# Queueing the last products behind the last transposes, and splitting the last row tile in three pieces, in a trace-of-product kernel

## The chip, the cores and the metric

One core of a Trainium2 chip runs the kernel. The metric is the device time of the whole program in microseconds (us); medians of repeated runs are quoted with their range. The profile of one execution is read beside them. Its own clock starts at the program's first instruction and its span is about 1.7 us shorter than the device time of the same execution. One caution for all that follows: the profiled execution of the kernel before took 712.63 us, and of its 31 timed runs (712.62 to 713.37) only one was faster. Its trace shows that kernel near its best.

## The reference

```python
def setup_inputs():
    B, N = 8, 2176
    return {"a": np.random.randn(B, N, N).astype(np.float32),
            "b": np.random.randn(B, N, N).astype(np.float32)}

def reference(a, b):
    prod = np.matmul(a, b)
    return np.diagonal(prod, axis1=1, axis2=2).sum(axis=-1).astype(np.float32)
```

Only the trace of each product is wanted: the sum over i and k of a[i, k] times b[k, i]. So nothing need be multiplied as matrices. A has to be transposed, and then a product element by element and a sum remain. The inputs are 303 MB, and each byte is read once.

## The kernel before

Both matrices are loaded in row groups (four row tiles of 128 rows to one transfer, and the seventeenth tile by itself), cast from fp32 to bf16 by the transfer. Only GpSimd ("POOL" in the profile) issues these casting loads here, 86 in all.

```python
    even = [ROWS] * (NT // ROWS) + [1] * (NT % ROWS)       # 4, 4, 4, 4, 1 row tiles
    fine = [4, 4, 4, 2, 1, 1, 1]                           # B of the last batch
    LAST_PIECES = [(0, 1, "PE"), (1, 2, "DVE"), (2, 3, "PE"), (3, 4, "DVE"), (4, 5, "DVE")]
    ...
    stage = ctx.enter_context(tc.tile_pool(name="stage", bufs=6))
    ...
    def load(src, start, m):
        t = stage.tile([P, ROWS, N], bf16, tag="stage")
        rows = src[start:start + P * m, :].rearrange("(p r) k -> p r k", r=m)
        nc.gpsimd.dma_start(out=t[:, 0:m, :], in_=rows)
        return t
```

A is transposed by TensorE into PSUM (the buffer that takes TensorE's results) and copied to the bf16 tile `at` by ScalarE (two of three copies) and VectorE. VectorE then multiplies each row tile of B with the matching rows of `at` and sums, with one instruction for a row (`multiply_reduce`; the profile names it CUSTOM_DVE). In the last batch, half of this goes to TensorE instead: it multiplies 128x128 blocks and accumulates them all in one PSUM tile, `trace_ps`. The diagonal of that is what is wanted, so at the end one more VectorE instruction multiplies it with the identity and sums it.

```python
    for bi in range(BATCH):
        ...
        for start, m in a_groups:
            a_t = load(a[bi], start, m)
            ...
            transpose_group(at, a_t, start, m, b_groups)
        ...
        for gi, (start, m) in enumerate(b_groups):
            v0 = start // P
            if last and gi == len(b_groups) - 1:          # the last row tile, in five pieces
                ...
                for g0, g1, _ in LAST_PIECES:
                    lo, hi = g0 * WIDE, min(g1 * WIDE, N)
                    nc.gpsimd.dma_start(out=row[:, lo:hi], in_=b[bi, start:start + P, lo:hi])
                ...
                continue
            b_t = load(b[bi], start, m)
            for s in range(m):
                row = b_t[:, s, :]
                if last and (m == 1 or s % 2 == 1):
                    ...                                    # TensorE: all of the row, or its second half
                else:
                    on_dve(wide_at(at, v0 + s, 0, n_wide), wide(row, 0, n_wide))
                    if last:
                        on_dve(at[:, v0 + s, split:], row[:, split:])   # 128 columns
        ...
    for n, (x, y) in enumerate(pe_work):
        nc.tensor.matmul(trace_ps, x, y, start=(n == 0), stop=(n == len(pe_work) - 1))
    multiply_reduce(late[0][0], late[0][1], late_acc[:, 0:1])
    multiply_reduce(late[1][0], late[1][1], late_acc[:, 1:2])
    multiply_reduce(tiles[f32], trace_ps, late_acc[:, 2:3])
    multiply_reduce(late[2][0], late[2][1], late_acc[:, 3:4])
    ...                                # sums over partitions on TensorE, copy, output DMA on SyncE
```

The order in which the source names the instructions is not the order in which an engine gets them: a scheduler decides that. It had put 16 of the products with B among the last transposes of A.

Of the kernel before, what the change touches and what calls it, by code (L numbers as in the profile page):

```python
# [10 lines left out]
def row_groups(p, rows):  # L11

    groups, at = [], 0
    for m in rows:
        groups.append((at, m))
        at += m * p
    return groups
# [3 lines left out]
def kernel(  # L21
# [6 lines left out]
    nc = tc.nc  # L28
    P = 128
    BATCH, N, N2 = a.shape  # L30
    assert N == N2 and N % P == 0
    NT = N // P
    ROWS = 4

    bf16 = mybir.dt.bfloat16
    f32 = mybir.dt.float32
# [4 lines left out]
    assert sum(even) == NT and sum(fine) == NT  # L41
    a_groups = row_groups(P, even)

    LAST_PIECES = [(0, 1, "PE"), (1, 2, "DVE"), (2, 3, "PE"), (3, 4, "DVE"), (4, 5, "DVE")]

    const = ctx.enter_context(tc.tile_pool(name="const", bufs=1))
    at_pool = ctx.enter_context(tc.tile_pool(name="at_pool", bufs=1))
# [12 lines left out]
    tiles = {}  # L60
# [16 lines left out]
    def evacuate(dst, src):  # L77
        nonlocal evacs
        if evacs % 3 == 2:
            nc.vector.tensor_copy(out=dst, in_=src)  # L80
        else:
            nc.scalar.copy(out=dst, in_=src)  # L82
        evacs += 1

    def multiply_reduce(x, y, acc):
        scratch = scratch_pool.tile([P, N], bf16, tag="scratch")
        out = scratch[:, :math.prod(x.shape[1:])]
        if len(x.shape) == 3:
            out = out.rearrange("q (a b) -> q a b", b=x.shape[2])
        elif len(x.shape) == 4:  # L90
            out = out.rearrange("q (a b c) -> q a b c", b=x.shape[2], c=x.shape[3])
        nc.vector.tensor_tensor_reduce(  # L92
            out=out, in0=x, in1=y, scale=1.0, scalar=0.0,
            op0=MUL, op1=ADD, accum_out=acc,
        )
# [3 lines left out]
    n_wide = NT // ROWS  # L99
    split = n_wide * WIDE  # L100

    def transpose_group(at, a_t, start, m, b_groups):

        words = a_t[:, :, :].bitcast(f32)
        g = start // WIDE
        if g < n_wide:
            dst = at[:, :, 0:split].rearrange("q v (r g p) -> q v g r p", r=m, p=P)[:, :, g, :, :]
        else:
            dst = at[:, :, split:].rearrange("q v (r p) -> q v r p", r=m)
        pairs, singles = [], []  # L110
        for b_start, bm in b_groups:
            v = b_start // P
            if bm % 2 == 0:
                for t in range(bm // 2):
                    pairs.append((v + 2 * t, b_start // 2 + t, bm // 2))
            else:
                singles.append((v, b_start))

        per_bank = 4 // m
        for at0 in range(0, len(pairs), per_bank):  # L120
            some = pairs[at0:at0 + per_bank]
            ps = psum_pool.tile([P, 4, P], f32, tag="aT")
            for n, (v, c0, step) in enumerate(some):
                for r in range(m):
                    nc.tensor.transpose(  # L125
                        ps[:, n * m + r, :],
                        words[:, r, c0:c0 + step * (P - 1) + 1:step],
                        tiles[f32],
                    )
            halves = ps.bitcast(bf16).rearrange("q (n r) (p s) -> q n s r p", r=m, s=2)  # L130
            v0 = some[0][0]
            if m == 1:
                evacuate(
                    dst[:, v0:v0 + 2 * len(some), 0, :].rearrange("q (n s) p -> q n s p", s=2),
                    halves[:, 0:len(some), :, 0, :],
                )
            else:
                assert len(some) == 1
                evacuate(dst[:, v0:v0 + 2, :, :], halves[:, 0, :, :, :])
        for at0 in range(0, len(singles), 8 // m):  # L140
            some = singles[at0:at0 + 8 // m]
            ps = psum_pool.tile([P, 4, P], f32, tag="aT")
            ps16 = ps.bitcast(bf16).rearrange("q a b -> q (a b)").rearrange("q (n r p) -> q n r p", r=m, p=P)
            for n, (v, c0) in enumerate(some):
                for r in range(m):
                    nc.tensor.transpose(  # L146
                        ps16[:, n, r, :],
                        a_t[:, r, c0:c0 + P],
                        tiles[bf16],
                    )  # L150
            v0 = some[0][0]
            evacuate(dst[:, v0:v0 + len(some), :, :], ps16[:, 0:len(some), :, :])

    def wide(row, g0, g1):

        return row[:, g0 * WIDE:g1 * WIDE].rearrange("q (x r) -> q r x", r=ROWS)

    def wide_at(at, v, g0, g1):
        block = at[:, v, 0:split].rearrange("q (r x) -> q r x", r=ROWS)
        return block[:, :, g0 * P:g1 * P]  # L160

    pe_work = []

    def multiply_on_pe(at, row, v, g0, g1):

        for start, m in a_groups[g0:g1]:
            for r in range(m):
                slot = r * n_wide + start // WIDE if m == ROWS else NT - m + r
                pe_work.append((
                    at[:, v, slot * P:(slot + 1) * P],  # L170
                    row[:, start + r:start + r + m * (P - 1) + 1:m],
                ))

    late = []
    for bi in range(BATCH):
        last = bi == BATCH - 1
        b_groups = row_groups(P, fine if last else even)


        at = at_pool.tile([P, NT, N], bf16, tag="at")  # L180
        for start, m in a_groups:
            a_t = load(a[bi], start, m)
            if not tiles:
                constants()
            transpose_group(at, a_t, start, m, b_groups)

        acc = acc_pool.tile([P, 2 * NT], f32, tag="acc")
        cols = 0

        def on_dve(x, y):  # L190
            nonlocal cols
            multiply_reduce(x, y, acc[:, cols:cols + 1])
            cols += 1

        for gi, (start, m) in enumerate(b_groups):
            v0 = start // P
            if last and gi == len(b_groups) - 1:
                b_t = stage.tile([P, ROWS, N], bf16, tag="stage")
                row = b_t[:, 0, :]
                for g0, g1, _ in LAST_PIECES:  # L200
                    lo, hi = g0 * WIDE, min(g1 * WIDE, N)
                    nc.gpsimd.dma_start(out=row[:, lo:hi], in_=b[bi, start:start + P, lo:hi])  # L202
                for g0, g1, engine in LAST_PIECES:
                    if engine == "PE":
                        multiply_on_pe(at, row, v0, g0, g1)
                    elif g0 < n_wide:
                        late.append((wide_at(at, v0, g0, g1), wide(row, g0, g1)))
                    else:
                        late.append((at[:, v0, split:], row[:, split:]))
                continue  # L210
            b_t = load(b[bi], start, m)
            for s in range(m):
                row = b_t[:, s, :]
                if last and (m == 1 or s % 2 == 1):
                    half = 2 if m == 1 else 0
                    multiply_on_pe(at, row, v0 + s, half, len(a_groups))
                    if half:
                        on_dve(wide_at(at, v0 + s, 0, half), wide(row, 0, half))
                else:
                    on_dve(wide_at(at, v0 + s, 0, n_wide), wide(row, 0, n_wide))  # L220
                    if last:
                        on_dve(at[:, v0 + s, split:], row[:, split:])
            if not last:
                on_dve(at[:, v0:v0 + m, split:], b_t[:, 0:m, split:])

        nc.vector.reduce_sum(  # L226
            out=tiles["sums"][:, bi:bi + 1], in_=acc[:, :cols], axis=mybir.AxisListType.X
        )


    trace_ps = psum_small.tile([P, P], f32, tag="trace")
    for n, (x, y) in enumerate(pe_work):
        nc.tensor.matmul(  # L233
            trace_ps, x, y, start=(n == 0), stop=(n == len(pe_work) - 1),
        )
    late_acc = tiles["late"]
    multiply_reduce(late[0][0], late[0][1], late_acc[:, 0:1])
    multiply_reduce(late[1][0], late[1][1], late_acc[:, 1:2])
    multiply_reduce(tiles[f32], trace_ps, late_acc[:, 2:3])
    multiply_reduce(late[2][0], late[2][1], late_acc[:, 3:4])  # L240

    total = psum_small.tile([1, BATCH], f32, tag="total")
    nc.tensor.matmul(
        total[:, 0:BATCH - 1], tiles["ones"], tiles["sums"][:, 0:BATCH - 1],
        start=True, stop=True,
    )
    parts = [tiles["sums"][:, BATCH - 1:BATCH]] + [late_acc[:, n:n + 1] for n in range(4)]
    for n, part in enumerate(parts):
        nc.tensor.matmul(  # L249
            total[:, BATCH - 1:BATCH], tiles["ones"], part,  # L250
            start=(n == 0), stop=(n == len(parts) - 1),
# [36 lines left out]
```

## Time and profile before

| quantity | before | where it is read |
|---|---|---|
| device time | 712.84 us (712.76 to 712.97, 3 runs) | runs |
| busy: TensorE, VectorE, ScalarE | 31%, 58%, 28% | first part of the page |
| DMA engines, bytes read | 90% or more in 39 of 40 slices; 303 MB, 426 GB/s | second and third part |
| TensorE standing for B in the middle of A's transposes | 22.0 us | waits |
| VectorE's first product of the last batch | 682.35 us | timeline |
| last load lands | 706.56 us | issue at 693.66, 12.9 us to landing |
| output issued, end of the span | 708.68, 710.87 us | timeline, span |

The kernel is bound by its transfers. These are lines of the second part of the page of the kernel before: the span in 40 slices, a digit for each, in tenths of busy time (9 is 90% or more), and the bytes that landed (half of those read, because of the cast).

```profile
...
PE   1460025600256003540035400364003630033195
...
DVE  0336982279822898218972199721996319951078
...
DMA  9999999999999999999999999999999999999997
GB/s 185 208 218 219 211 224 214 213 219 211 225 213 215 218 218 218 216 213 217 219 218 215 212 218 218 219 215 213 216 218 218 216 214 216 218 218 214 218 213 137
...
```

The DMA row is full to the last slice, and the rate is even. A pause of TensorE or VectorE costs nothing by itself as long as the transfers go on.

The waits of the kernel before, from 640 us on (engine and line, what it waited for: us in total, times, longest):

```profile
...
POOL t L57 <- PE ps L146: 49.3, 4, 33.8
...
PE trace_ps L233 <- DMA t<-in_b_dram: 26.3, 5, 22.0
...
```

TensorE stood 22.0 us for B's first group, with transposes of A queued behind (the Trainium skill, "TensorE: Matmul & The Clock Gate", Part 3, says that matmuls are strictly in order; this agrees: the first of the 16 products ahead of the last transposes held them up for these 22.0 us), and POOL could issue no load for 33.8 us, since the buffer that it wanted was still to be transposed. The timeline of the end (start, duration, instruction, in brackets the engine's idle time before it and what ended that):

```profile
...
672.77 0.39 PE L233 MATMUL trace_ps<-t,at 128*128 128x128 bf16 x2 [22.04 <-DMA t<-in_b_dram]
...
682.35 2.28 DVE L92 CUSTOM_DVE_ANT_1 scratch<-at,t 128x2048 bf16<-128x2048 bf16 x1
...
693.66 0.53 POOL L202 DMA_DIRECT2D b_t<-in_b_dram  x1 [1.14 <-DMA t<-in_b_dram]
...
707.59 0.29 DVE L92 CUSTOM_DVE_ANT_0 scratch<-identity,trace_ps 128x128 bf16<-128x128 f32 x1 [0.18 <-DVE late L92]
...
707.92 0.29 DVE L92 CUSTOM_DVE_ANT_0 scratch<-at,b_t 128x128 bf16<-128x128 bf16 x1
...
708.50 0.15 DVE L253 COPY result<-total 1x8 f32<-1x8 f32 x1 [0.28 <-PE total L249]
708.68 0.31 SPq L254 DMA_DIRECT2D out_dram<-result  x1
```

The landing of the last piece is read from the page's last part (size, and us from issue to landing):

```profile
...
b_t<-in_b_dram POOLq DMA_DIRECT2D x1, 32.0 KB, 12.9
...
```

Issued at 693.66, it landed at 706.56. VectorE starts its first product 9.6 us after its data landed (672.73) and stays busy. After the last piece's product (707.92) come the sums on TensorE, the copy and the output's issue at 708.68; behind it, 2.2 us to the end of the span.

### The profile page before, as it was taken

The page shows a single profiled execution, that of the slowest core. Times are in us where ns is not written, and L with a number is a line of the kernel's source. Part 1 is how long each engine was busy: PE and PEld are TensorE (multiplying, and loading weights), DVE is VectorE, ACT ScalarE, POOL GpSimd, SP SyncE. Part 2 cuts the span into 40 slices and gives each one's busy share as a digit, 9 for nine tenths or more (in the row PEclk, how much of TensorE's full clock was granted, in tenths as well). Part 3 has the DMA queues.
Part 4 walks back from the last instruction along what each step waited for, and adds up shares of the span by engine and source line. Part 5 has one row for each costly group of instructions (what it writes and reads, how often), then busy time and mean ns, then how long its engine had stood idle before and what let it go on. Part 6 is the DMA issues. An engine that isn't in the chain of part 4 may idle for free.

```text
span 710.9 us, 3799 instructions
## 1 busy us (share of the span) xinstructions
PE 222.7 (31%) x1398; PEld 210.8 (30%) x1398; DVE 410.0 (58%) x462; ACT 199.5 (28%) x209; POOL 46.6 (7%) x94
## 2 busy tenths in 40 slices
PE   1460025600256003540035400364003630033195
PEld 1460024600256003540035400364003630033185
DVE  0336982279822898218972199721996319951078
ACT  1561015600156002450034500354003630033060
POOL 2000000000000000000000000000000000000020
PEclk9985558855567555885558855567556875566596
DMA  9999999999999999999999999999999999999997
GB/s 185 208 218 219 211 224 214 213 219 211 225 213 215 218 218 218 216 213 217 219 218 215 212 218 218 219 215 213 216 218 218 216 214 216 218 218 214 218 213 137
DMA packets 12404, 151.76 MB, mean 213 GB/s; under 512 B 1506, under 2 KB 2018, under 8 KB 4194
## 3 DMA queue, kind: packets, MB, share of 16 engines
q0 software_dynamic: 12384, 151.52, 100.5%
q8 instruction: 11, 0.18, 0.1%
q14 instruction: 7, 0.06, 0.0%
q1 hardware_dynamic: 2, 0.00, 0.0%
HBM read 303.04 MB, written 0.00 MB: 426 GB/s over the span
## 4 chain that ended last, share of the span: by engine, by line
DMA 48%; issue 43%; DVE 3%; POOL 2%; PE 2%; another core or an unknown queue 1%; POOLq 0%; DVEq 0%
DMA t<-in_a_dram 42%; DMA t<-in_b_dram 6%; DVE scratch L92 3%; POOL t L57 2%; PE ps L125 2%; DVE at L80 0%; PE trace_ps L233 0%; PE ps L146 0%; POOLq L57 0%; DVE acc L92 0%; POOL identity masks.py:199 0%; POOL identity masks.py:197 0%; DVE late L92 0%; PE total L249 0%
## 5 line engine op out<-in xcount | busy, mean ns | idle before, releaser
L92 DVE CUSTOM_DVE_ANT_1 scratch<-at,t 128x2048 bf16<-128x2048 bf16 (+1 forms) x156 | 310.5, 1990 | 66.3 <-DMA t<-in_b_dram 60.0
L125 PE MATMUL ps<-identity,t 128*128 128x128 f32 x1071 | 195.0, 359 | 456.1 <-DMA t<-in_a_dram 355.8
L82 ACT COPY at<-ps 128x1024 bf16<-128x1024 bf16 x208 | 198.2, 1019 | 487.1 <-PE ps L125 486.9
L125 PEld LDWEIGHTS ps<-identity,t 128*128 128x128 f32 x1071 | 183.9, 217 | 464.4 <-issue 361.0
L80 DVE COPY at<-ps 128x1024 bf16<-128x1024 bf16 (+2 forms) x104 | 92.4, 901 | 230.1 <-PE ps L125 225.2
L57 POOL DMA_DIRECT2D t<-in_b_dram x41 | 21.7, 529 | 320.2 <-PE ps L146 305.3
L57 POOL DMA_DIRECT2D t<-in_a_dram x40 | 21.3, 533 | 323.0 <-DVE acc L92 245.4
L233 PE MATMUL trace_ps<-t,at 128*128 128x128 bf16 x137 | 17.0, 291 | 26.3 <-DMA t<-in_b_dram 26.3
L233 PEld LDWEIGHTS <-at 128*128 128x128 bf16 x145 | 16.4, 118 | 27.5 <-issue 27.1
L146 PE MATMUL ps<-identity,t 128*128 128x128 bf16 x170 | 16.7, 222 | 2.1 <-DVE at L80 2.1
L146 PEld LDWEIGHTS <-t 128*128 128x128 bf16 x170 | 13.3, 102 | 3.6 <-issue 3.2
L92 DVE DVE_READ_ACCUMULATOR2_ANT acc<- 128x1 f32 x170 | 13.8, 81 | 0.0
L92 DVE CUSTOM_DVE_ANT_0 scratch<-at,t 128x128 bf16<-128x128 bf16 x14 | 4.1, 291 | 0.6
L202 POOL DMA_DIRECT2D b_t<-in_b_dram x5 | 2.6, 540 | 4.1 <-issue 3.0
L226 DVE TENSOR_REDUCE sums<-acc 128x1 f32<-128x22 f32 (+1 forms) x8 | 1.4, 175 | 0.3
L82 ACT ACT_TABLE_LOAD x1 | 1.3, 1283 | 0.7 <-PEq L272 0.7
L92 DVE CUSTOM_DVE_ANT_1 scratch<-at,b_t 128x512 bf16<-128x512 bf16 x2 | 1.4, 687 | 0.0
L233 PE MATMUL trace_ps<-b_t,at 128*128 128x128 bf16 x8 | 1.2, 295 | 0.0
L249 PE MATMUL total<-late,ones 128*1 128x1 f32 x8 | 0.8, 164 | 1.2 <-DVE late L92 1.1
L249 PEld LDWEIGHTS total<-late,ones 128*1 128x1 f32 x8 | 0.3, 81 | 1.6 <-DVE late L92 1.6
masks.py:199 POOL TENSOR_SCALAR_AFFINE_SELECT identity<-identity 128x128 f32<-128x128 f32 (+1 forms) x2 | 0.5, 302 | 0.0
L68 DVE MEMSET ones<- 128x1 f32 x1 | 0.1, 59 | 0.8 <-PEq L272 0.8
(13 smaller groups left out, 2.4 us busy)
## 6 DMA issues: line engine op xcount, KB each, us to landing
t<-in_a_dram POOLq DMA_DIRECT2D x32, 2176.0 KB, 42.3
t<-in_b_dram POOLq DMA_DIRECT2D x31, 2176.0 KB, 47.3
t<-in_b_dram POOLq DMA_DIRECT2D x9, 544.0 KB, 39.9
t<-in_a_dram POOLq DMA_DIRECT2D x8, 544.0 KB, 35.0
t<-in_b_dram POOLq DMA_DIRECT2D x1, 1088.0 KB, 18.8
b_t<-in_b_dram POOLq DMA_DIRECT2D x4, 128.0 KB, 14.2
b_t<-in_b_dram POOLq DMA_DIRECT2D x1, 32.0 KB, 12.9
out_dram<-result SPq DMA_DIRECT2D x1, 0.0 KB
```

The lines of the kernel that those rows point to most:

```text
L57: nc.gpsimd.dma_start(out=t[:, 0:m, :], in_=rows)
L68: nc.vector.memset(ones, 1.0)
L80: nc.vector.tensor_copy(out=dst, in_=src)
L82: nc.scalar.copy(out=dst, in_=src)
L92: nc.vector.tensor_tensor_reduce(out=out, in0=x, in1=y, scale=1.0, scalar=0.0, op0=MUL, op1=ADD, accum_out=acc,)
L125: nc.tensor.transpose(ps[:, n * m + r, :], words[:, r, c0:c0 + step * (P - 1) + 1:step], tiles[f32],)
L146: nc.tensor.transpose(ps16[:, n, r, :], a_t[:, r, c0:c0 + P], tiles[bf16],)
L202: nc.gpsimd.dma_start(out=row[:, lo:hi], in_=b[bi, start:start + P, lo:hi])
L226: nc.vector.reduce_sum(out=tiles["sums"][:, bi:bi + 1], in_=acc[:, :cols], axis=mybir.AxisListType.X)
L233: nc.tensor.matmul(trace_ps, x, y, start=(n == 0), stop=(n == len(pe_work) - 1),)
L249: nc.tensor.matmul(total[:, BATCH - 1:BATCH], tiles["ones"], part, start=(n == 0), stop=(n == len(parts) - 1),)
```

## The change

Three things are meant. All products on TensorE are queued behind the last transpose, so that no transpose waits for B. The last row tile comes in three pieces in place of five, and TensorE and VectorE share each of them. The 128-column rest of each row moves from VectorE (a reduction for each row) to TensorE (one product each).

```diff
-    LAST_PIECES = [(0, 1, "PE"), (1, 2, "DVE"), (2, 3, "PE"), (3, 4, "DVE"), (4, 5, "DVE")]
+    LAST_PIECES = [(0, 2), (2, 3), (3, 5)]
 ... (transpose_group returns its last transpose; multiply_on_pe takes the number of rows)
-                for g0, g1, engine in LAST_PIECES:
-                    if engine == "PE":
-                        multiply_on_pe(at, row, v0, g0, g1)
-                    elif g0 < n_wide:
-                        late.append((wide_at(at, v0, g0, g1), wide(row, g0, g1)))
-                    else:
-                        late.append((at[:, v0, split:], row[:, split:]))
+                multiply_on_pe(at, row, v0, 0, 1)
+                late.append((wide_at(at, v0, 1, 2), wide(row, 1, 2)))
+                for g in range(2, n_wide):
+                    half = ROWS // 2
+                    multiply_on_pe(at, row, v0, g, g + 1, rows=half)
+                    late.append((
+                        wide_at(at, v0, g, g + 1)[:, half:, :], wide(row, g, g + 1)[:, half:, :]
+                    ))
+                multiply_on_pe(at, row, v0, n_wide, len(a_groups))
 ...
                     if last:
-                        on_dve(at[:, v0 + s, split:], row[:, split:])
+                        multiply_on_pe(at, row, v0 + s, n_wide, len(a_groups))
 ...
-    for n, (x, y) in enumerate(pe_work):
-        nc.tensor.matmul(
-            trace_ps, x, y, start=(n == 0), stop=(n == len(pe_work) - 1),
-        )
+    with tc.issue_after(last_transpose.ins):
+        for n, (x, y) in enumerate(pe_work):
+            nc.tensor.matmul(
+                trace_ps, x, y, start=(n == 0), stop=(n == len(pe_work) - 1),
+            )
 ... (late products in a loop; the identity's product after them, not before the last)
```

More of the change, by code (lines that the diff above doesn't have):

```diff
@@ L145, in transpose_group @@
                 for r in range(m):
-                    nc.tensor.transpose(
+                    last_transpose = nc.tensor.transpose(
                         ps16[:, n, r, :],
@@ L152, in transpose_group @@
             evacuate(dst[:, v0:v0 + len(some), :, :], ps16[:, 0:len(some), :, :])
+        return last_transpose
     def wide(row, g0, g1):
@@ L162, with multiply_on_pe @@
     pe_work = []
-    def multiply_on_pe(at, row, v, g0, g1):
+    def multiply_on_pe(at, row, v, g0, g1, rows=ROWS):
         for start, m in a_groups[g0:g1]:
-            for r in range(m):
+            for r in range(min(m, rows)):
                 slot = r * n_wide + start // WIDE if m == ROWS else NT - m + r
@@ L184 @@
                 constants()
-            transpose_group(at, a_t, start, m, b_groups)
+            last_transpose = transpose_group(at, a_t, start, m, b_groups)
         acc = acc_pool.tile([P, 2 * NT], f32, tag="acc")
@@ L199 @@
                 row = b_t[:, 0, :]
-                for g0, g1, _ in LAST_PIECES:
+                for g0, g1 in LAST_PIECES:
                     lo, hi = g0 * WIDE, min(g1 * WIDE, N)
                     nc.gpsimd.dma_start(out=row[:, lo:hi], in_=b[bi, start:start + P, lo:hi])
-                for g0, g1, engine in LAST_PIECES:
-                    if engine == "PE":
-                        multiply_on_pe(at, row, v0, g0, g1)
-                    elif g0 < n_wide:
-                        late.append((wide_at(at, v0, g0, g1), wide(row, g0, g1)))
-                    else:
-                        late.append((at[:, v0, split:], row[:, split:]))
+                multiply_on_pe(at, row, v0, 0, 1)
[7 more added lines that the diff above has]
+                multiply_on_pe(at, row, v0, n_wide, len(a_groups))
                 continue
@@ L231 @@
     trace_ps = psum_small.tile([P, P], f32, tag="trace")
-    for n, (x, y) in enumerate(pe_work):
-        nc.tensor.matmul(
-            trace_ps, x, y, start=(n == 0), stop=(n == len(pe_work) - 1),
-        )
+    with tc.issue_after(last_transpose.ins):
[3 more added lines that the diff above has]
+            )
     late_acc = tiles["late"]
-    multiply_reduce(late[0][0], late[0][1], late_acc[:, 0:1])
-    multiply_reduce(late[1][0], late[1][1], late_acc[:, 1:2])
-    multiply_reduce(tiles[f32], trace_ps, late_acc[:, 2:3])
-    multiply_reduce(late[2][0], late[2][1], late_acc[:, 3:4])
+    for n, (x, y) in enumerate(late):
+        multiply_reduce(x, y, late_acc[:, n:n + 1])
+    multiply_reduce(tiles[f32], trace_ps, late_acc[:, len(late):len(late) + 1])
     total = psum_small.tile([1, BATCH], f32, tag="total")
@@ L246 @@
     )
-    parts = [tiles["sums"][:, BATCH - 1:BATCH]] + [late_acc[:, n:n + 1] for n in range(4)]
+    parts = [tiles["sums"][:, BATCH - 1:BATCH]] + [late_acc[:, n:n + 1] for n in range(len(late) + 1)]
     for n, part in enumerate(parts):
```

## The prediction

> **What bounds the kernel now.** The transfers. The page shows the 16 DMA engines at 90% or more in every slice but the last (mean 97 to 100%), 303 MB read at 426 GB/s; TensorE is busy 31% of the span, VectorE 58%, ScalarE 28%. Only the end, after the last bytes, can be shortened by rearranging compute.
>
> **The end now.** The timeline of the last 60 us shows TensorE reaching the first product of batch 7's B rows at 650.3 us, in the middle of the transposes of A's third wide group, and standing 22.0 us until the first B group lands at 672.8. The transposes behind it run only from 672.9 to 686.4; the next B load is issued only at 679.7 (POOL waited 33.8 us for a transpose). This agrees with the Trainium skill, "TensorE: Matmul & The Clock Gate" (Part 3: matmuls are strict FIFO). VectorE starts its first last-batch reduction at 682.35, 9.6 us after its data came, and is then busy practically without a gap until 708.2; TensorE and output follow to 710.9. But the queue never ran dry meanwhile: the stretches from 655 to 690 move about 205 to 244 GB/s, so the 33.8 us of POOL waiting cost no transfer time. The B tiles reach TensorE at 693.4, 698.6, 701.2 and 704.1, and the last piece lands at about 706.6 (issue at 693.66 plus 12.9 us). So VectorE is only some 1.6 us behind the transfers at the end, despite starting 9.6 us late. That bounds the gain.
>
> **What changes.** The order of instructions puts all 145-odd products behind the last transpose, so A's last two groups are transposed on arrival (about 660 to 663; a few evacuations stay behind VectorE's first reduction, which waits for 672.7, so they end near 677). VectorE then starts 9 to 10 us sooner, and loses seven 128-wide reductions (0.33 us each with the accumulator read and gap, 2.3 us in all). It will therefore wait for B tiles instead of lagging. From then on the end is:
> - last full row tile lands 704.1; VectorE's half of it 1.22 + 0.1; the sum over columns 0.17: 705.6
> - 512-wide piece 0.69 + 0.1: 706.4
> - two 256-wide halves, estimated from the 128-, 512- and 1024-wide durations (0.29, 0.69, 1.22) at 0.42 + 0.1 each: 707.3
> - identity times the products 0.29 + 0.1: 707.7, against 708.2 now.
>
> The pieces go from five to three. The narrow 256-byte rows of the last piece go out at 30 to 60 GB/s in the DMA view of the end; the merge may save 0.3 to 0.5 us of landing (estimate), so the last piece should land near 706.2 and not be the last wait. TensorE gets 17 more products (about 0.12 us each, 2 us) which it has time for; only three follow the last piece.
>
> **Prediction.** 0.3 to 1.0 us of 712.84: 712.2 us, range 711.4 to 712.9. Faster by over 2%: 0.01; within 2%: 0.98; slower by over 2%: 0.01.
>
> **What would show it.** Right: no wait of TensorE's products for B ahead of an A transpose; POOL's 33.8 us wait gone, bytes per slice unchanged up to 690; VectorE idle for several us, waiting for B, between 675 and 703; first B tile still landing near 672.7; last-row reductions starting near 705.6. Wrong: a shift of the B landings (then the queue's depth does matter to its rate), VectorE still busy without a gap from 672 on, or the chain ending in a wait of the last identity product for TensorE.
>
> **What would make it wrong.** Deeper queueing could move the B landings by a microsecond either way; the larger first piece may land late and hold VectorE; a change of more than 2% would need the transfers themselves to change, and their bytes are the same.

## The result, and the profile after

| | before | after |
|---|---|---|
| device time, same rounds | 712.80 us (712.75 to 712.97, 4 runs) | 712.52 us (712.47 to 712.80, 4 runs) |
| last load lands | 706.56 | 706.55 |
| output issued | 708.68 | 708.05 |
| end of the profile's span | 710.87 | 710.77 |

The ratio is 0.9996, with a 95% interval of 0.9979 to 1.0014: the same within 2%, and the runs alone do not tell the kernels apart. (A ratio is the mean time of one kernel's runs over that of the other's runs of the same rounds, so it is not quite the ratio of the medians.) The traces show more than the times do, but the 0.10 us between the two spans is probably too small, since the trace before is of a fast execution. These are the lines of the page after that answer to those of before:

```profile
...
PE   1570025700245003540036500364003630036356
...
DVE  0236982279822898218972199721996319953146
...
DMA  8999999999999999999999999999999999999997
GB/s 183 212 216 219 211 224 213 215 218 212 225 212 217 218 217 220 214 212 219 218 218 214 212 219 218 218 217 209 219 218 218 217 209 219 218 218 215 216 212 139
...
```

The waits from 640 us on, after:

```profile
...
POOL t L57 <- PE ps L146: 40.0, 4, 11.3
...
DVE scratch L92 <- DMA t<-in_b_dram: 21.3, 6, 9.5
...
PE trace_ps L237 <- DMA t<-in_b_dram: 10.2, 5, 6.1
...
```

and the timeline of the end, after:

```profile
...
673.01 2.29 DVE L92 CUSTOM_DVE_ANT_1 scratch<-at,t 128x2048 bf16<-128x2048 bf16 x1 [9.51 <-DMA t<-in_b_dram]
...
676.51 0.92 PE L125 MATMUL ps<-identity,t 128*128 128x128 f32 x3 [10.07 <-DVE at L80]
...
683.30 2.29 DVE L92 CUSTOM_DVE_ANT_1 scratch<-at,t 128x2048 bf16<-128x2048 bf16 x1 [4.04 <-DMA t<-in_b_dram]
...
706.67 0.43 DVE L92 CUSTOM_DVE_ANT_1 scratch<-at,b_t 128x256 bf16<-128x256 bf16 x1 [0.19 <-DMA b_t<-in_b_dram]
...
707.29 0.29 DVE L92 CUSTOM_DVE_ANT_0 scratch<-identity,trace_ps 128x128 bf16<-128x128 f32 x1 [0.18 <-PE total L252]
...
707.87 0.15 DVE L256 COPY result<-total 1x8 f32<-1x8 f32 x1 [0.28 <-PE total L252]
708.05 0.31 SPq L257 DMA_DIRECT2D out_dram<-result  x1
```

The chain of waits after has the last landing as a piece (start, us, what); it ends at 706.55:

```profile
...
683.17 23.37 DMA b_t<-in_b_dram
...
706.59 0.50 PE trace_ps L237 x3
...
```

TensorE's 22 us and POOL's 33.8 us are gone. VectorE starts its first product at 673.01, 9.3 us sooner, and now stands for B (21.3 us in all) in place of lagging behind it. The output is issued 0.63 us sooner. And yet the span is 0.10 us shorter. What became of the other half microsecond is hidden in records that the page does not count as work: those of the program's closing barrier (the point at which each engine waits for all others), which carry the line of the launch code (L283 before, L286 after). First POOL's, then SyncE's, of the kernel before (operation, count, ns minimum/median/maximum, first and last start in us):

```profile
...
L283 POOLq DRAIN  x1: 16477/16477/16477, 693.6 to 693.6; - x1
...
```

```profile
...
L283 SPq EVENT_SEMAPHORE  x6: 17/28/28, 709.0 to 709.8; - x6
L283 SPq DRAIN  x2: 7/7/7, 709.8 to 709.9; - x2
...
```

and of the changed kernel:

```profile
...
L286 POOLq DRAIN  x1: 27051/27051/27051, 683.0 to 683.0; - x1
...
```

```profile
...
L286 SPq EVENT_SEMAPHORE  x6: 17/28/28, 708.4 to 709.1; - x6
L286 SPq DRAIN  x2: 7/7/7, 709.2 to 709.2; - x2
...
```

POOL's DRAIN follows its loads; its record starts about when the last of them is issued (693.64 and 693.66 before, 682.97 and 683.17 after). Before, it runs from 693.64 for 16.48 us, to 710.12. After, it runs from 682.97 for 27.05 us, to 710.02. SyncE has waited for the output's landing and is ready for the barrier at 709.9 before, and at 709.25 after. In both kernels POOL is the last to arrive at the barrier. So 0.22 us of the output's path lay in the shade of POOL's drain before, and 0.77 us do now; the change shortened a path that was not the last one. Subtracting the landing gives 3.56 us from the last landing to the end of the drain before, and 3.47 us after.

### The profile page after: what moved, and what is told of

It is laid out like the page before. It is cut to its first block, busy times and chain, and to the rows that moved or that the text cites. A ratio compares the mean times of both kernels' runs of the same rounds, so it can differ in the third digit from the quotient of the medians.

```text
span 710.8 us, 3799 instructions
## 1 busy us (share of the span) xinstructions
PE 228.6 (32%) x1406; PEld 217.1 (31%) x1406; DVE 407.9 (57%) x448; ACT 200.3 (28%) x209; POOL 45.5 (6%) x92
## 3 DMA queue, kind: packets, MB, share of 16 engines
q0 software_dynamic: 12096, 151.52, 100.4%
## 4 chain that ended last, share of the span: by engine, by line
DMA 51%; issue 42%; POOL 3%; PE 2%; DVE 1%; another core or an unknown queue 1%; POOLq 0%; DVEq 0%
DMA t<-in_a_dram 42%; DMA t<-in_b_dram 6%; DMA b_t<-in_b_dram 3%; POOL t L57 2%; PE ps L125 1%; PE trace_ps L237 1%; DVE scratch L92 0%; DVE at L80 0%; POOL b_t L203 0%; POOLq L57 0%; POOL identity masks.py:199 0%; PE ps L146 0%; PE total L252 0%; POOL identity masks.py:197 0%
## 5 line engine op out<-in xcount | busy, mean ns | idle before, releaser
L125 PE MATMUL ps<-identity,t 128*128 128x128 f32 x1071 | 199.6, 366 | 465.6 <-DMA t<-in_a_dram 317.7
L125 PEld LDWEIGHTS ps<-identity,t 128*128 128x128 f32 x1071 | 189.1, 218 | 473.6 <-issue 362.6
L57 POOL DMA_DIRECT2D t<-in_a_dram x40 | 21.3, 533 | 321.4 <-DVE acc L92 245.0
L92 DVE CUSTOM_DVE_ANT_0 scratch<-at,t 128x128 bf16<-128x128 bf16 x7 | 2.0, 291 | 0.2
L92 DVE CUSTOM_DVE_ANT_1 scratch<-at,b_t 128x256 bf16<-128x256 bf16 (+1 forms) x3 | 1.5, 511 | 0.2 <-DMA b_t<-in_b_dram 0.2
```

The source lines that it names most:

```text
L92: nc.vector.tensor_tensor_reduce(out=out, in0=x, in1=y, scale=1.0, scalar=0.0, op0=MUL, op1=ADD, accum_out=acc,)
L125: nc.tensor.transpose(ps[:, n * m + r, :], words[:, r, c0:c0 + step * (P - 1) + 1:step], tiles[f32],)
```

## The experiments

All kernels are the changed kernel with one edit, unless said otherwise. Theory 1, formed on the two traces above: the end hangs on POOL's drain, and that on the last landing. Theory 2, the rival and the prediction's own assumption: the end follows the output at a fixed distance. The device times of the kernel before in the three sets of rounds had medians of 712.87, 712.95 and 712.95 us. Every run of this section is "the same within 2%" as the kernel before, so the argument rests on the traces, and on differences of time that stand out from the ranges given.

### The compute of the end taken away, made longer, made shorter

`load_only` (batch 7's sum is wrong) loads the last row tile as ever but multiplies it with nothing:

```diff
+                continue
                 multiply_on_pe(at, row, v0, 0, 1)
```

> The changed kernel with its last row tile loaded as ever but used by nobody (batch 7's sum is wrong on purpose), so the output is issued near 706.3 us instead of 708.05. Theory 1 (the end of the span hangs on POOL's final drain, which ends about 3.5 us after the last load of its queue has landed; in both kernels 710.1 and 710.0, with SyncE ready at 709.9 and 709.25): the last landing stays at 706.5, the drain at 710.0, and the time stays within 0.2 us of the changed kernel, 712.4 to 712.7. Theory 2 (the end follows the output DMA at a fixed distance of 2.2 to 2.7 us): 1.7 us shorter, about 710.8.

Measured: 712.63 us (712.55 to 712.72). The output was issued at 706.19 us, 1.86 us sooner than in the changed kernel, and SyncE was ready near 707.4; the last landing was at 706.62, POOL's drain ended at 710.09, and the span was 710.84:

```profile
...
L287 POOLq DRAIN  x1: 27058/27058/27058, 683.0 to 683.0; - x1
...
```

Taking away all compute behind the last landing gains nothing. Theory 2 is wrong by 1.8 us.

`no_last` (wrong too) leaves out the three loads as well, with the same compute as in `load_only`:

```diff
             if last and gi == len(b_groups) - 1:
+                continue
```

> As load_only, but the three loads of the last row tile are left out too (wrong on purpose). The compute behind is the same as in load_only. Theory 1: last landing about 703.9, so POOL's drain ends near 707.4, and the end moves with it or with the output (issued near 706.2, SyncE ready near 707.4): span about 708.2, time about 710.0, 2.5 us below load_only. Theory 2: the time equals that of load_only within 0.3 us, because the output is issued at the same moment.

Measured: 710.01 us (709.93 to 710.25). The output was issued at 706.31, practically as in `load_only`, but the last landing was at 704.03 and POOL's drain ended at 707.38, 3.35 us later:

```profile
...
L287 POOLq DRAIN  x1: 29183/29183/29183, 678.2 to 678.2; - x1
...
```

With SyncE ready at 707.50, the span ended at 708.23. Two kernels with outputs 0.1 us apart ended 2.6 us apart.

`long1` and `long6` do the identity's product once or six times more ahead of the real one:

```diff
+    extra = const.tile([P, 8], f32, tag="extra")
+    for n in range(1):                          # 6 in long6
+        multiply_reduce(tiles[f32], trace_ps, extra[:, n:n + 1])
     multiply_reduce(tiles[f32], trace_ps, late_acc[:, len(late):len(late) + 1])
```

> The changed kernel with the product of the identity and the PSUM sums done once more ahead of the real one, about 0.35 to 0.45 us more on the chain to the output (results right). Theory 1: SyncE is ready at 709.65 instead of 709.25, still ahead of POOL's drain at 710.0: time unchanged within 0.1 us, 712.5. Theory 2: 0.4 us more, 712.9.

> The same with six extra products, 2.1 to 2.6 us more on the chain to the output. Theory 1: SyncE is ready near 711.5, POOL's drain no longer matters; of the 2.3 us the first 0.75 is hidden, so 1.4 to 1.8 us more: about 714.1. Theory 2: all of it shows: about 714.8.

Measured: 712.63 us (712.60 to 712.69) for `long1`, whose output was issued at 708.47, 0.42 us later than in the changed kernel, with SyncE ready at 709.64 and the drain ending at 710.11. `long6` took 713.77 us (713.69 to 713.97): output at 710.23, 2.18 us later, SyncE ready at 711.44, drain over at 710.23, span 712.17. Of the 2.18 us, 1.40 show in the span; the rest was slack. The end comes 0.73 to 0.76 us after the later one of SyncE and POOL, in all these traces.

### Which part of the change did what

`order_only` is the kernel before with nothing but the ordering:

```diff
+    with tc.issue_after(last_transpose.ins):
         for n, (x, y) in enumerate(pe_work):
             nc.tensor.matmul(...)
```

> The kernel before with only the products queued behind the last transposes; five pieces as before. TensorE's 22.0 us wait and POOL's 33.8 us wait should go, VectorE should wait for B like in the changed kernel. Output issued near 708.2 us (VectorE: 512-wide products of pieces two and four, identity, 128-wide piece after the last landing at 706.55). Theory 1 (POOL's drain, last landing plus 3.35 to 3.56 us, decides): time within 0.15 us of both kernels, 712.5 to 712.9, and the drain ends at 710.0 to 710.1. Theory 2 (how far VectorE lags decides): 0.4 to 0.6 us faster than before.

Measured: 712.71 us (712.68 to 712.87). TensorE's longest wait for B fell from 22.0 to 6.3 us and POOL's longest for a transpose from 33.8 to 10.7, and VectorE waited for B. The output was issued at 708.60, 0.08 us sooner than before. VectorE now waits for the last full row of B, which landed at 704.42, and from there it does the same work as before without a pause, the last piece having long landed (706.71) when its product starts (707.84). In the kernel before, VectorE had lagged 0.53 us behind that row (landed 704.10, product from 704.63). The ordering took the lag away, but the row landed 0.32 us later, and only 0.08 us were left. First the kernel before, then `order_only`:

```profile
...
704.63 1.22 DVE L92 CUSTOM_DVE_ANT_1 scratch<-at,t 128x1024 bf16<-128x1024 bf16 x1
...
704.55 1.23 DVE L92 CUSTOM_DVE_ANT_1 scratch<-at,t 128x1024 bf16<-128x1024 bf16 x1 [1.55 <-DMA t<-in_b_dram]
...
```

The drain ended 3.55 us after the landing (706.71), as before. In the traces the ordering by itself brought nothing (span 711.00 against 710.87). In the same rounds its median is 0.24 us below that of the kernel before (712.95); the interval of the ratio, 0.9985 to 1.0010, includes one, and no trace shows where such a gain would come from.

`pieces_only` is the changed kernel without the ordering:

```diff
-    with tc.issue_after(last_transpose.ins):
-        for n, (x, y) in enumerate(pe_work):
+    for n, (x, y) in enumerate(pe_work):
             nc.tensor.matmul(...)
```

> The changed kernel without its ordering: three pieces, the products of the one-row column group on TensorE, but the products queued among the transposes again. TensorE waits 22 us and POOL 33.8 us as before; VectorE starts at 682.4 again, but has seven 128-wide reductions (2.3 us) less to do, so it catches up with the transfers by the last B tiles: output issued within 0.3 us of 708.05. Theory 1: last landing 706.55, drain 710.0, time 712.5 to 712.7. If the deeper queue of the new order mattered, the landing here would be later than 706.6; I expect it is not.

Measured: 712.64 us (712.48 to 712.70); output at 708.05, last landing 706.55, drain to 710.02, all as in the changed kernel. But the waits that I expected back did not come: TensorE's longest was 6.2 us. The trace explains it: its 1406 TensorE products and transposes come in the same order as the changed kernel's. A product with the 128-column rest, which reads the last transposed group of A, now stands among the first products, and all products accumulate in one tile, which is probably why the scheduler put them behind the last transpose without being told. This kernel is thus a repeat of the changed one, and no test of the ordering; `order_only` is. The 0.55 us between `order_only` (708.60) and this one (708.05) belong to the pieces and the moved rests. In part they come from the transfers: the last full row, whose load was issued at the same moment (678.06 and 678.03), landed at 704.42 with five pieces behind it and at 703.84 with three.

### What POOL's drain waits for

`hw_piece` loads the last piece (640 columns) in fp32 on SyncE's queue, when the last full row of B has landed, and reduces it on VectorE alone. A one-column copy on POOL gives the signal:

```diff
-    LAST_PIECES = [(0, 2), (2, 3), (3, 5)]
+    LAST_PIECES = [(0, 2), (2, 3)]
 ...
+                row32 = const.tile([P, N - 3 * WIDE], f32, tag="row32")
+                with tc.issue_after(issued.ins):
+                    nc.gpsimd.tensor_copy(out=row32[:, 0:1], in_=singles_of_b[-1][:, 0, 0:1])
+                nc.sync.dma_start(out=row32, in_=b[bi, start:start + P, 3 * WIDE:])
+                ...                              # its two products on VectorE, after the identity's
```

> The changed kernel with its last piece (640 columns) loaded in fp32 by SyncE's queue instead of POOL's, issued when the last full B row has landed (a one-column copy on POOL gives the signal), and reduced by VectorE alone; results right. POOL's own queue then lands its last load near 705.8. Theory 1a (the drain follows the last landing of POOL's own queue): the drain ends near 709.3, and SyncE (output issued near 708.6, ready near 709.8) decides: span about 710.5, time 712.2 to 712.4. Theory 1b (the drain follows the last landing of any load): it ends 3.4 us after the SyncE load has landed, near 710.1 or later, and the time is no better than 712.5.

Measured: 713.44 us (713.38 to 713.79). The drain ended at 710.97, which neither form of the theory said: 5.17 us after the last landing of POOL's queue (705.80), 3.87 us after SyncE's load (707.10). The copy had delayed the drain's start to 703.90, and `pool_touch`, in the same set, shows that this matters.

`pool_touch` adds only a one-column copy on POOL that waits for the last piece:

```diff
+    touch = const.tile([P, 1], bf16, tag="touch")
+    nc.gpsimd.tensor_copy(out=touch, in_=row[:, N - 1:N])
```

> The changed kernel with one more POOL instruction after its last issue, a one-column copy that waits for the last piece to land (706.55), so that the drain itself begins near 706.7 instead of 683. If the 3.4 us after the landing belong to the queue, the drain still ends near 710.0 and the time stays at 712.5. If the drain sleeps or polls in growing steps from its start, its end will move (either way, by up to some us).

Measured: 716.28 us (716.16 to 716.63), 3.8 us slower than the changed kernel (span 714.55 against 710.77), for one copy of 0.19 us:

```profile
...
L288 POOLq DRAIN  x1: 7156/7156/7156, 706.6 to 706.6; - x1
...
```

A drain that starts with everything landed (706.65; the last landing was 706.62) takes 7.16 us. In `hw_piece` it took 7.07 us from its start. So two conditions hold: it needs some 7.1 us from its start, and 3.5 us from the last landing. In the kernel before and in the changed one it starts soon enough for the first not to matter.

`touch_b3` is the control, with the copy waiting for a tile of B that lands at 698.7:

```diff
+                touch = const.tile([P, 1], bf16, tag="touch")
+                with tc.issue_after(issued.ins):
+                    nc.gpsimd.tensor_copy(out=touch, in_=loaded[-3][:, 0, 0:1])
```

> Control for pool_touch: the same kind of one-column POOL copy after the last issue, but of the two-row B tile, which lands at 698.7, so the drain begins near 698.9 instead of 683 or 706.65. If a drain needs about 7.1 us from its start (as 706.65 to 713.80 and 703.90 to 710.97 say) or 3.47 us from the last landing, whichever ends later: 698.9 + 7.1 is 706.0, so it ends at 710.0 and the time is 712.5. If a POOL instruction ahead of the drain is itself what made it slow: time 714 or more.

Measured: 712.65 us (712.55 to 712.87).

```profile
...
L290 POOLq DRAIN  x1: 11329/11329/11329, 698.7 to 698.7; - x1
...
```

The drain ended at 710.03, 3.47 us after the landing at 706.56. The copy is harmless; a drain that starts late is not.

`hw_piece2` repeats `hw_piece` with the signal as a small DMA on SyncE's own queue:

```diff
-                with tc.issue_after(issued.ins):
-                    nc.gpsimd.tensor_copy(out=row32[:, 0:1], in_=singles_of_b[-1][:, 0, 0:1])
-                nc.sync.dma_start(out=row32, in_=b[bi, start:start + P, 3 * WIDE:])
+                signal = const.tile([1, 256], bf16, tag="signal")
+                signal = nc.sync.dma_start(out=signal, in_=singles_of_b[-1][0:1, 0, 0:256])
+                with tc.issue_after(signal.ins):
+                    nc.sync.dma_start(out=row32, in_=b[bi, start:start + P, 3 * WIDE:])
```

> As hw_piece (last piece in fp32 on SyncE's queue, after the last full B row has landed), but the signal is a small DMA on SyncE's own queue and not a POOL copy, so the drain begins near 682.7 again and its own 7.1 us cannot hide the answer. Last landing of POOL's queue near 705.8, of the SyncE load near 707.5. If the drain waits for POOL's own queue alone: end near 709.2. If for every load: near 710.9 to 711. SyncE (output near 709.4, ready near 710.6) then sets the end or nearly: time 713.0 to 713.5, no better version, but the drain's end decides.

Measured: 713.39 us (713.34 to 713.67). POOL's last load landed at 706.04, SyncE's at 707.94, and the drain ended at 709.48: 3.44 us after POOL's own, 1.5 us after the other. The drain, and SyncE's load (KB, and us from its issue at 704.76 to landing):

```profile
...
L296 POOLq DRAIN  x1: 26942/26942/26942, 682.5 to 682.5; - x1
...
row<-in_b_dram SPq DMA_DIRECT2D x1, 320.0 KB, 3.2
...
```

The drain waits for POOL's own queue alone. The version is slower because SyncE's load landed late and its products came on top: output at 709.93.

### Why 3.5 us

The landing-to-end times so far are 3.35 us with 81 loads on POOL's queue (`no_last`), 3.47 with 84 and 3.55 to 3.56 with 86. Divided by the number of loads, that is 0.0413 us each time. Two kernels test this in both directions.

`more_dmas` puts 24 loads of 128 values each, which nobody reads, into the first half of the queue:

```diff
         nc.gpsimd.dma_start(out=t[:, 0:m, :], in_=rows)
+        if 10 <= len(counted) < 34:
+            tiny = const.tile([1, 128], bf16, tag=f"tiny{len(counted)}")
+            nc.gpsimd.dma_start(out=tiny, in_=src[0:1, 0:128])
+        counted.append(t)
```

> The changed kernel with 24 tiny loads (128 values of one row each, into tiles that nobody reads) scattered over the first half of POOL's queue: 108 DMAs, but only 24 rows more. Theory A (per DMA): landing to end of drain 108 times 0.0413, 4.46 us instead of 3.47, so 1.0 us more in the time, if the last landing stays: 713.5. Theory B (per packet or last loads): 3.5 us, time 712.5 to 712.8.

Measured: 714.41 us (714.23 to 714.62). The last landing came 0.7 us later (707.26), and the drain ended at 711.71, 4.45 us after it.

```profile
...
L292 POOLq DRAIN  x1: 28088/28088/28088, 683.6 to 683.6; - x1
...
```

`fewer3` loads the one-row groups of three batches with one DMA, for A and for B:

```diff
+    def load_single(src, name, bi, start, upto):
+        if bi % 3 == 0:
+            n = min(3, upto - bi)
+            t = pairs.tile([P, 3, N], bf16, tag=name)
+            nc.gpsimd.dma_start(
+                out=t[:, 0:n, :], in_=src[bi:bi + n, start:start + P, :].rearrange("b p k -> p b k")
+            )
+            several[name] = t
+        return several[name][:, bi % 3:bi % 3 + 1, :]
...
-            a_t = load(a[bi], start, m)
+            a_t = load(a[bi], start, m) if m > 1 else load_single(a, "a1", bi, start, BATCH)
...
-            b_t = load(b[bi], start, m)
+            b_t = load(b[bi], start, m) if m > 1 or last else load_single(b, "b1", bi, start, BATCH - 1)
```

> The changed kernel with the one-row column groups of up to three batches loaded by one DMA each (A: 8 loads become 3, B: 7 become 3), so POOL's queue has 75 DMAs instead of 84; the same bytes, results right. So far the time from the last landing to the end of POOL's drain was 3.35 us with 81 DMAs, 3.47 with 84 and 3.55 with 86: 0.0413 us for each DMA of the whole run. Theory A (the drain walks over every DMA of the queue): 75 times 0.0413 is 3.10 us, 0.37 less; span 710.4, time 712.1 to 712.3, the best of all. Theory B (the 3.5 us depend on the packets or the last loads alone): 3.4 to 3.5 us, time 712.5. A stall of the prefetch would show as a later last landing and is told apart by it.

Measured: 712.20 us (712.11 to 712.24), against 712.95 (712.62 to 713.37) for the kernel before in the same rounds. The last landing stayed at 706.53, and the drain ended 3.10 us later, at 709.63:

```profile
...
L299 POOLq DRAIN  x1: 26734/26734/26734, 682.9 to 682.9; - x1
...
```

It is the fastest correct kernel: its range lies below those of both kernels, and its span (710.38) is 0.39 us shorter than the changed kernel's, with the output issued at the same moment (708.03). It is still 0.1%: the ratio to the kernel before is 0.9989, and the interval, 0.9976 to 1.0001, just includes one. It was not run in the same rounds as the changed kernel. SyncE is ready at 709.21 there, 0.42 us ahead of the drain, so about ten loads more could be saved (an estimate, 0.42 over 0.0413) before the output's path decides.

All drains together, from the traces (times in us; "to end" is from the last landing of POOL's queue to the end of the drain, good to 0.01):

| kernel | loads on POOL's queue | last landing | drain starts | drain ends | to end | SyncE ready | span |
|---|---|---|---|---|---|---|---|
| before | 86 | 706.56 | 693.64 | 710.12 | 3.56 | 709.90 | 710.87 |
| after | 84 | 706.55 | 682.97 | 710.02 | 3.47 | 709.25 | 710.77 |
| order_only | 86 | 706.71 | 693.78 | 710.26 | 3.55 | 709.79 | 711.00 |
| load_only | 84 | 706.62 | 683.03 | 710.09 | 3.47 | 707.4 | 710.84 |
| long1 | 84 | 706.64 | 683.05 | 710.11 | 3.47 | 709.64 | 710.85 |
| pieces_only | 84 | 706.55 | 682.83 | 710.02 | 3.47 | 709.25 | 710.77 |
| touch_b3 | 84 | 706.56 | 698.70 | 710.03 | 3.47 | 709.23 | 710.78 |
| no_last | 81 | 704.03 | 678.19 | 707.38 | 3.35 | 707.50 | 708.23 |
| long6 | 84 | 706.76 | 683.13 | 710.23 | 3.47 | 711.44 | 712.17 |
| hw_piece2 | 83 | 706.04 | 682.53 | 709.48 | 3.44 | 711.16 | 711.90 |
| more_dmas | 108 | 707.26 | 683.62 | 711.71 | 4.45 | 709.97 | 712.47 |
| fewer3 | 75 | 706.53 | 682.90 | 709.63 | 3.10 | 709.21 | 710.38 |
| hw_piece | 83 | 705.80 | 703.90 | 710.97 | 5.17 (7.07 from start) | 710.32 | 711.71 |
| pool_touch | 84 | 706.62 | 706.65 | 713.80 | 7.18 (7.16 from start) | 709.3 | 714.55 |

Theory A, a cost for each load of the whole run, holds at 75, 81, 83, 84, 86 and 108 loads, with 0.0413 us. Theory B falls twice: by the page's DMA part the queue moved 12,096 packets in the changed kernel, 12,864 in `more_dmas` (6% more, but 28% more drain) and 11,952 in `fewer3` (1% fewer, but 11% less drain). `hw_piece2` moved the same 11,952 packets as `fewer3`, with 83 loads, and needed 3.44 us. The queue's packets, MB and share of the DMA engines' span, in this order:

```profile
...
q0 software_dynamic: 12096, 151.52, 100.4%
...
q0 software_dynamic: 12864, 151.53, 100.3%
...
q0 software_dynamic: 11952, 151.52, 100.5%
...
```

That the drain walks through a list of the queue's loads, and must do so once more after the last landing, fits the numbers (the 7.16 and 7.07 us from the start are 0.0852 us for each load, about twice 0.0413), but no run looks inside it, and the time from the start was seen with 83 and 84 loads only.

## Why the prediction was right, and where it was off

The measured 712.52 us lie in the range of 711.4 to 712.9, and "within 2%" was given 0.98. The point, 712.2, promised 0.6 us; the medians give 0.28, and the spans of the traces 0.10. The range took in the 712.84 us of the kernel before, so it would have held with no gain at all; that the number came out right is partly luck, since the way in which the prediction meant to gain is not the one that shows in the traces.

- **"What bounds the kernel now": right.** The DMA row stayed full between its first and last slices, and the first B tile landed at 672.89 after 672.73.
- **"The 33.8 us of POOL waiting cost no transfer time": right.** The wait is gone, the last pieces are issued 23 us ahead of their landing instead of 13 to 14, and the last one lands at 706.55 instead of 706.56.
- **VectorE starts "9 to 10 us sooner" and then waits for B: right** (9.3 us; 21.3 us of waiting). As `order_only` shows, this by itself moved the output by 0.08 us. The prediction had seen that VectorE was hardly behind at the end, and was right to make little of the large waits.
- **The steps of the end: right to 0.4 us.** Predicted were 705.6, 706.4, 707.3 and 707.7 for the column sum, the 512-wide product, the two halves and the identity's product; they ended at 705.4, 706.0, 707.1 and 707.6. The output came 0.63 us sooner, which is the gain that the prediction had in mind. One thing that it had named as a sign of being wrong is there: the chain of waits reaches the identity's product through TensorE's three last products (706.59 to 707.09). It cost next to nothing, since VectorE's own last product ended at 707.10.
- **"TensorE and output follow to 710.9": the step that failed.** It took the 2.2 us from the output to the end as a fixed distance, so that each tenth gained before the output would be gained at the end. The end hung on POOL's drain, 3.56 us after the last landing before and 3.47 after. SyncE was already 0.22 us ahead of the drain in the kernel before, so nothing gained ahead of the output could show. In the traces the span's 0.10 us are the drain's: the landing gave 0.02, and two loads fewer on the queue give 2 times 0.0413, or 0.08. The rest of the difference between the medians (0.28 against 0.10) stays open. It is small, but it came back in the same rounds: `load_only`, `long1`, `pieces_only` and `touch_b3` lie 0.24 to 0.31 us below the kernel before, and `order_only`, with as many loads as the kernel before, 0.24. None of their intervals excludes a ratio of one, and the profiled execution of the kernel before, one of its fastest, cannot show where it comes from.
- **"The merge may save 0.3 to 0.5 us of landing": wrong.** The last landing moved by 0.02 us, and it was the last wait of the data after all (VectorE 0.19 us and TensorE 0.37 us, to 706.55), not at rest by 706.2. The merge paid nonetheless, in the number of loads, and in the last full row, which landed at 703.85 instead of 704.10.
- **"TensorE gets 17 more products": a miscount.** It gets 8 more, 153 in place of 145. It had the time for either.

## What to carry to other kernels

Before costing a gain at the end of a kernel, read what lies between the last instruction that touches data and the end of the span, and find the participant that comes last to the closing barrier: here it was the engine that issues the loads, which had had nothing to do for 27 us. Where GpSimd issues the loads and its drain comes last, as here, count them, let its last instruction come early, and merge small loads even if the transfers themselves gain nothing. And a long wait is worth only what is left of it at the next point where its engine waits for the transfers anyway: two waits of 22 and 34 us were removed here, and the output came 0.08 us sooner. One trace of each kernel is not enough for differences of this size; look at where the profiled execution lies among the timed ones.

## What the Trainium skill lacked or had wrong

- The skill's page "DMA: Bandwidth & Descriptors" (Rules for kernel authors) advises to coalesce many small transfers into a large one, because a transfer under 64 KB is mostly overhead. The run with 24 tiny loads agrees: they moved the last landing by 0.7 us, although at the 213 GB/s of the page their 6 KB would take 0.03 us (an estimate). No page says that each load issued by GpSimd is paid for once more at the end: here 0.0413 us per load of the run from the last landing to the end of POOL's drain (3.10 us with 75 loads, 4.45 us with 108). Nor does one say what a drain costs that starts late: 7.16 us with 84 loads, 7.07 us with 83.
- "VectorE: DVE Perf Modes" (The DRAIN you can't avoid) tells the pipeline flush of VectorE from a boilerplate DRAIN of about 12 ns on all engines. SyncE's here are of that size (7 ns), but the DRAIN that follows POOL's loads is of neither kind: it lasted 7.1 to 29.2 us, and in most of these kernels it sets the end of the span.
- "Perfetto Trace Analysis" (Sequencer-only Instruction) says that a DRAIN's record holds only its execution and not the time it waits for semaphores. What it lacks is that the execution can itself be a wait: POOL's record of 27.05 us shows no semaphore, and its end moved with the last landing (710.02 against 707.38 us with the last loads left out).
